# Two landing buffers each for q, k and v, requested two units ahead, in a windowed attention kernel on Trainium2

## Chip, cores and metric

One core of a Trainium2 chip. The metric is the time of one execution on the device in microseconds, measured without the profiler; smaller is better. "Before" ran in 947.35 us (median of the four runs beside the changed kernel, 946.81 to 947.8).

## The reference

Attention inside windows of 64 rows. No window sees another.

```python
B, S, D, W = 4, 4096, 1536, 64           # q, k, v: (B, S, D) float32
q_w = q.reshape(B, S // W, W, D)         # k_w, v_w the same way
logits = einsum('bnwd,bnud->bnwu', q_w, k_w) * D ** -0.5
attn = softmax(logits, axis=-1)
out = einsum('bnwu,bnud->bnwd', attn, v_w)
```

Inputs and output are 100.66 MB each, 402.65 MB in all. There is little arithmetic for each byte.

## The kernel before

The 16,384 rows are cut into N = 32 units of 512 rows (4 row slots on 128 partitions). For each unit q, k and v are loaded by GpSimd with a cast from float32 to float16 on the way, 3.146 MB read each; TensorE transposes q and k, multiplies, ScalarE takes the exponential, TensorE multiplies by v, VectorE and ScalarE scale into one of three output buffers, and GpSimd requests the store, 3.146 MB. A load lands in a landing buffer; GpSimd then copies it into `q16`, `k16` or `v16` ("hand over"), so that the landing buffer is free while TensorE works. `m_q` counts the units whose q has been transposed.

```python
ql = sb("ql", [P, SLOTS, D], FP16)            # one landing buffer for q
kl = sb("kl", [P, SLOTS, D], FP16)            # one for k
NV = 2
vls = [sb(f"vl{i}", [P, SLOTS, D], FP16) for i in range(NV)]   # two for v
# ... cut
def hand_over(src, dst, d, u, m, g):          # GpSimd
    gp.wait_ge(d, 16 * u)                     # landed
    gp.wait_ge(m, copies[0] // 3 + 1)         # dst no longer read
    gp.tensor_copy(out=dst..., in_=src...).then_inc(c_l, 1)
    copies[0] += 1
    gp.wait_ge(c_l, copies[0])
    gp.sem_inc(g, 1)                          # TensorE may start
# ... cut: SyncE requests q of unit 0 in three parts (row slot 0, slot 1, slots 2 and 3)
nc.gpsimd.wait_ge(d_r0, 16)                   # row slot 0 of q has landed
nc.gpsimd.affine_select(out=ident...)
load("k", 0, k16, d_k0)
load("v", 0, v16, d_v0)
# ... cut: q of unit 0 cast on GpSimd, q1, k1, v1, v2 requested
for u in range(1, N):
    hand_over(ql, q16, d_q, u, m_q, g_q)
    if u + 1 < N:
        load("q", u + 1, ql, d_q)
    hand_over(kl, k16, d_k, u, m_k, g_k)
    if u + 1 < N:
        load("k", u + 1, kl, d_k)
    for what in {N - 3: "", N - 2: "-v"}.get(u, "s"):      # the tail has its own order
        if what == "v":
            load("v", N - 1, vls[(N - 1) % NV], d_v[(N - 1) % NV])
        else:
            gp.wait_ge(m_q, u + 1)
            store(u - 2 if what == "-" else u - 1)
    if u == N - 2:
        store(u - 1)
    hand_over(vls[u % NV], v16, d_v[u % NV], (u + u % NV) // NV, m_v, g_v)
    if u + NV < N - 1:
        load("v", u + NV, vls[u % NV], d_v[u % NV])
# the last unit's store in two halves: one from GpSimd, one from SyncE
for h, (eng, c) in enumerate(((gp, 1), (sy, 3))):
    # ... cut: waits
    eng.dma_start(out=..., in_=...).then_inc(d_l[h], 16)
gp.drain()
# ... cut: SyncE waits for the last landings, GpSimd clears the semaphores
```

The softmax here doesn't subtract the row's maximum and nothing guards it: scores larger than these inputs give would overflow.

## Time and profile before

| | before |
|---|---|
| time | 947.35 us (median) |
| span of the profiled run | 946.4 us |
| DMA engines busy | 90% or more in 39 of 40 slices |
| TensorE, VectorE, ScalarE, GpSimd busy | 69%, 30%, 35%, 36% |
| HBM traffic | 402.65 MB, 425 GB/s over the span |

Read it from the DMA row: the engines that move the bytes hardly ever rest, those that compute do. The prediction below shows the slices and the timeline and divides the span by them. Three groups of instructions belong beside it, GpSimd's copies at the hand-overs (busy us in all, mean ns, then the idle time before them and what ended it):

```profile
L292 POOL COPY q<-ql 128x3072 f32<-128x3072 f32 x31 | 85.0, 2743 | 395.7 <-DMA ql<-in_q_dram 395.5
...
L292 POOL COPY k<-kl 128x3072 f32<-128x3072 f32 x31 | 85.3, 2751 | 110.5 <-DMA kl<-in_k_dram 110.5
...
L292 POOL COPY v<-vl 128x3072 f32<-128x3072 f32 x31 | 85.5, 2758 | 10.4 <-DMA vl<-in_v_dram 10.4
```

and the DMA issues (size, then the median time from the issue to the landing in us):

```profile
out_dram<-out POOLq DMA_DIRECT2D x31, 3072.0 KB, 32.5
ql<-in_q_dram POOLq DMA_DIRECT2D x31, 1536.0 KB, 25.8
kl<-in_k_dram POOLq DMA_DIRECT2D x31, 1536.0 KB, 25.8
vl<-in_v_dram POOLq DMA_DIRECT2D x31, 1536.0 KB, 35.7
```

GpSimd waits 395.5 us for q. That is the number that invites the change.

### The profile page before, as it was taken

The numbers are of one execution on the slowest core, as the hardware profiler recorded it, in microseconds if no ns is written. First come the engines' busy times: TensorE is split into PE (matmuls) and PEld (weight loads), VectorE is DVE, ScalarE is ACT, GpSimd is POOL, SyncE is SP. The second block draws the span as 40 slices with busy tenths as digits, with TensorE's granted clock in tenths as the row PEclk, the third lists the DMA queues.
The fourth block names the chain that finished last, engine by engine and source line by source line (L and its number), as shares of the span: only waits on it lengthen the run. The fifth ranks groups of instructions, "written<-read, shape, count | busy, mean of one in ns | idle before, by whom it ended". The sixth has DMA issues, their size and how long they took to land. (4 is left out here: it accounts for less than half of the span.)

```text
span 946.4 us, 11421 instructions
## 1 busy us (share of the span) xinstructions
PE 651.0 (69%) x4096; PEld 419.8 (44%) x3456; DVE 279.7 (30%) x453; ACT 332.8 (35%) x642; POOL 341.5 (36%) x229
## 2 busy tenths in 40 slices
PE   2776866768667676667777667866768666777682
PEld 2544543445534345434554344543435533445450
DVE  1333223332233231333313323223322233232331
ACT  1433323333334342333423334323333234343252
POOL 4323343233442334423344323343233442333520
PEclk9989777897878887798878789878898879797897
DMA  9999999999999999999999999999999999999997
GB/s 250 216 229 270 283 281 282 242 257 283 281 280 258 243 282 282 278 270 236 278 282 280 279 238 265 282 280 282 249 251 283 283 281 264 238 279 283 197 315 321
DMA packets 26940, 253.35 MB, mean 268 GB/s; under 512 B 2096, under 2 KB 2096, under 8 KB 10544
## 3 DMA queue, kind: packets, MB, share of 16 engines
q0 software_dynamic: 26352, 248.52, 100.0%
q1 hardware_dynamic: 576, 4.72, 1.3%
q14 instruction: 10, 0.08, 0.0%
q8 instruction: 2, 0.03, 0.0%
HBM read 301.99 MB, written 100.66 MB: 425 GB/s over the span
## 5 line engine op out<-in xcount | busy, mean ns | idle before, releaser
L147 PE MATMUL tp<-ident,q 128*128 128x128 f32 x768 | 165.0, 384 | 185.6 <-PEq L213 172.7
L147 PEld LDWEIGHTS tp<-ident,q 128*128 128x128 f32 x768 | 131.2, 200 | 239.4 <-issue 236.8
L292 POOL COPY q<-ql 128x3072 f32<-128x3072 f32 x31 | 85.0, 2743 | 395.7 <-DMA ql<-in_q_dram 395.5
L159 PE MATMUL lt<-xq,xk 128*128 128x256 f16 x1536 | 210.2, 288 | 0.0
L147 PE MATMUL tp<-ident,k 128*128 128x128 f32 x768 | 136.3, 317 | 67.3 <-PEq L213 54.5
L159 PEld LDWEIGHTS lt<-xq,xk 128*128 128x128 f16 x1536 | 156.8, 102 | 30.4
L222 ACT COPY xq<-tp 128x512 f32<-128x512 f32 x96 | 60.2, 627 | 291.2 <-ACTq L213 291.2
L147 PEld LDWEIGHTS tp<-ident,k 128*128 128x128 f32 x768 | 105.1, 163 | 86.3 <-issue 83.9
L222 DVE COPY xq<-tp 128x512 f32<-128x512 f32 x96 | 66.4, 692 | 254.7 <-DVEq L213 254.7
L222 ACT COPY xk<-tp 128x512 f32<-128x512 f32 x96 | 59.8, 623 | 228.6 <-ACTq L213 228.6
L222 DVE COPY xk<-tp 128x512 f32<-128x512 f32 x96 | 66.5, 693 | 198.6 <-DVEq L213 198.6
L292 POOL COPY k<-kl 128x3072 f32<-128x3072 f32 x31 | 85.3, 2751 | 110.5 <-DMA kl<-in_k_dram 110.5
L264 ACT ACTIVATE et<-lt,zeros 32x128 f16<-32x128 f32 x256 | 92.0, 359 | 39.4 <-ACTq L213 36.1
L188 PEld LDWEIGHTS <-et 128*128 128x128 f16 x384 | 30.2, 97 | 152.7 <-issue 116.7
L115 PE MATMUL o<-v,et 128*128 128x512 f16 x384 | 93.3, 379 | 0.0
L251 DVE TENSOR_SCALAR out<-o,rs 128x512 f32<-128x512 f32 x128 | 90.2, 747 | 7.7
L292 POOL COPY v<-vl 128x3072 f32<-128x3072 f32 x31 | 85.5, 2758 | 10.4 <-DMA vl<-in_v_dram 10.4
L115 PE MATMUL tp<-v,et 128*128 128x512 f16 x256 | 75.8, 377 | 0.0
L241 DVE RECIPROCAL rs<-sp 128x2 f32<-128x2 f32 x64 | 10.6, 166 | 162.6 <-DVEq L213 162.4
L275 ACT ACTIVATE out<-tp,rs 128x512 f32<-128x512 f32 x64 | 44.0, 688 | 37.2 <-ACTq L213 31.3
L251 DVE TENSOR_SCALAR out<-tp,rs 128x512 f32<-128x512 f32 x64 | 48.1, 751 | 26.2 <-DVEq L213 26.2
L115 PE MATMUL lt<-v,et 128*128 128x512 f16 x128 | 48.3, 377 | 0.0
(22 smaller groups left out, 201.2 us busy)
## 6 DMA issues: line engine op xcount, KB each, us to landing
out_dram<-out POOLq DMA_DIRECT2D x31, 3072.0 KB, 32.5
ql<-in_q_dram POOLq DMA_DIRECT2D x31, 1536.0 KB, 25.8
kl<-in_k_dram POOLq DMA_DIRECT2D x31, 1536.0 KB, 25.8
vl<-in_v_dram POOLq DMA_DIRECT2D x31, 1536.0 KB, 35.7
out<-in_q_dram SPq DMA_DIRECT2D x2, 768.0 KB, 6.5
out<-in_q_dram SPq DMA_DIRECT2D x1, 1536.0 KB, 11.2
k<-in_k_dram POOLq DMA_DIRECT2D x1, 1536.0 KB, 12.2
v<-in_v_dram POOLq DMA_DIRECT2D x1, 1536.0 KB, 18.8
```

Of the source, the lines that this page charges most:

```text
L115: return nc.tensor.add_instruction(mybir.InstMatmult(name=nc.get_next_instruction_name(), engine=PE, ins=[low(rhs), low(w)], outs=[low(o)] ...
L147: ins = nc.tensor.transpose(tps[g % 2][:, r, j, :], pairs[:, c * P : (c + 1) * P], ident[:, :])
L159: ins = nc.tensor.matmul(lts[h][:, r, :, :], lhsT=halves(xk, c)[:, r, h, :, w], rhs=halves(xq, c)[:, :, h, :, w], start=(c == 0 and w == 0 ...
L188: ld = nc.tensor.ldweights(w)
L222: copy(out=dst, in_=tps[g % 2][:, :, :, :]).then_inc(f_c[g % 4], 1)
L241: ve.reciprocal(out=rs[:, n : n + R], in_=sp[:, n : n + R]).then_inc(n_d, 1)
L251: ins = ve.tensor_scalar_mul(scaled(u, n, j), bank(n, j), scalar1=rs[:, n : n + 1])
L264: ins = sc.activation(ets[h][s, :, :, s], lts[h][s, :, :, s], EXP, bias=zeros[s, 0:1], scale=scale)
L275: ins = sc.activation(scaled(u, n, j), bank(n, j), COPY, bias=0.0, scale=rs[:, n : n + 1])
L292: gp.tensor_copy(out=dst[:, :, :].bitcast(FP32), in_=src[:, :, :].bitcast(FP32)).then_inc(c_l, 1)
```

## The change

The intent: q and k get a second landing buffer, as v has, so that a request never waits for its own buffer; with it all requests go out two units ahead in one plain order (q, k, store, v), and the tail's own order is dropped. In addition the very first transfer is half a row slot, so that GpSimd can request k and v of unit 0 sooner. Two more buffers of 12 KiB per partition are used. The core of the diff:

```diff
-    ql = sb("ql", [P, SLOTS, D], FP16)
-    kl = sb("kl", [P, SLOTS, D], FP16)
-    NV = 2
-    vls = [sb(f"vl{i}", [P, SLOTS, D], FP16) for i in range(NV)]
+    NL = 2
+    landing = {x: [sb(f"{x}l{i}", [P, SLOTS, D], FP16) for i in range(NL)] for x in "qkv"}
...
+    def request(x, u):
+        if u < N:
+            load(x, u, landing[x][u % NL], landed[x][u % NL])
...
     # hand_over(x, u, dst, m, g): waits for landed[x][u % NL], copies, and at its end:
+        request(x, u + NL)
...
-        for sl, s in ((slice(0, 1), d_r0), (slice(1, 2), d_r1), (slice(2, SLOTS), d_r2)):
-            nc.sync.dma_start(out=outs[0][:, sl, :], in_=raw[:, sl, :]).then_inc(s, 16)
+        for lo, hi, c0, c1, s in (
+            (0, 1, 0, D // 2, d_r0), (0, 1, D // 2, D, d_r1), (1, 2, 0, D, d_r2), (2, SLOTS, 0, D, d_r3)
+        ):
+            nc.sync.dma_start(
+                out=outs[0][:, lo:hi, c0:c1], in_=raw[:, lo:hi, c0:c1]
+            ).then_inc(s, 16)
...
+        for x, u in (("k", 1), ("v", 1), ("q", 2), ("k", 2), ("v", 2)):
+            request(x, u)
...
         for u in range(1, N):
+            hand_over("q", u, q16, m_q, g_q)
+            hand_over("k", u, k16, m_k, g_k)
+            gp.wait_ge(m_q, u + 1)
+            store(u - 1)
+            hand_over("v", u, v16, m_v, g_v)
     # (the loop body of before, with the tail's own order, is removed)
```

More of the change, by code (lines that the diff above doesn't have):

```diff
@@ L74 @@
     sp = ps("sp", [P, 4])
-    d_r0, d_r1, d_r2, d_q, d_k, d_k0, d_v0 = (
-        sem(n) for n in ("d_r0", "d_r1", "d_r2", "d_q", "d_k", "d_k0", "d_v0")
+    d_r0, d_r1, d_r2, d_r3, d_k0, d_v0 = (
+        sem(n) for n in ("d_r0", "d_r1", "d_r2", "d_r3", "d_k0", "d_v0")
     )
-    d_v = [sem(f"d_v{i + 1}") for i in range(NV)]
+    landed = {x: [sem(f"d_{x}{i + 1}") for i in range(NL)] for x in "qkv"}
     d_o = [sem(f"d_o{i}") for i in range(NO)]
@@ L283, in store, with hand_over @@
         ).then_inc(d_o[u % NO], 16)
+    def request(x, u):
+        if u < N:
+            load(x, u, landing[x][u % NL], landed[x][u % NL])
     copies = [0]
-    def hand_over(src, dst, d, u, m, g):
+    def hand_over(x, u, dst, m, g):
         gp = nc.gpsimd
-        gp.wait_ge(d, 16 * u)
-        gp.wait_ge(m, copies[0] // 3 + 1)
+        gp.wait_ge(landed[x][u % NL], 16 * ((u + u % NL) // NL))
+        gp.wait_ge(m, u)
         gp.tensor_copy(
-            out=dst[:, :, :].bitcast(FP32), in_=src[:, :, :].bitcast(FP32)
+            out=dst[:, :, :].bitcast(FP32), in_=landing[x][u % NL][:, :, :].bitcast(FP32)
         ).then_inc(c_l, 1)
@@ L314 @@
         for i in range(SLOTS):
-            nc.gpsimd.wait_ge((d_r0, d_r1, d_r2, d_r2)[i], 16)
+            nc.gpsimd.wait_ge((d_r1, d_r2, d_r3, d_r3)[i], 16)
             nc.gpsimd.tensor_copy(out=q16[:, i, :], in_=outs[0][:, i, :]).then_inc(c_q, 1)
             if i == 1:
-                load("q", 1, ql, d_q)
-        load("k", 1, kl, d_k)
-        for u in range(1, NV + 1):
-            load("v", u, vls[u % NV], d_v[u % NV])
+                request("q", 1)
+        for x, u in (("k", 1), ("v", 1), ("q", 2), ("k", 2), ("v", 2)):
+            request(x, u)
         nc.vector.memset(ones[:, :], 1.0).then_inc(i_d, 1)
@@ L358 @@
         for u in range(1, N):
-            hand_over(ql, q16, d_q, u, m_q, g_q)
-            if u + 1 < N:
-                load("q", u + 1, ql, d_q)
-            hand_over(kl, k16, d_k, u, m_k, g_k)
-            if u + 1 < N:
-                load("k", u + 1, kl, d_k)
-            for what in {N - 3: "", N - 2: "-v"}.get(u, "s"):
-                if what == "v":
-                    load("v", N - 1, vls[(N - 1) % NV], d_v[(N - 1) % NV])
-                else:
-                    gp.wait_ge(m_q, u + 1)
-                    store(u - 2 if what == "-" else u - 1)
-            if u == N - 2:
-                store(u - 1)
-            hand_over(vls[u % NV], v16, d_v[u % NV], (u + u % NV) // NV, m_v, g_v)
-            if u + NV < N - 1:
-                load("v", u + NV, vls[u % NV], d_v[u % NV])
+            hand_over("q", u, q16, m_q, g_q)
[3 more added lines that the diff above has]
+            hand_over("v", u, v16, m_v, g_v)
         base, o = (N - 1) * UR, outs[(N - 1) % NO]
```

## The prediction

> **What bounds the kernel now.** I read the page's slices first, then its DMA part, then GpSimd's timeline, because GpSimd issues nearly every transfer, and last the landing records.
>
> The slices of the span (tenths busy; DMA is the mean over the 16 DMA engines), then the DMA queues and the HBM traffic:
>
> ```profile
> PE   2776866768667676667777667866768666777682
> POOL 4323343233442334423344323343233442333520
> DMA  9999999999999999999999999999999999999997
> ...
> q0 software_dynamic: 26352, 248.52, 100.0%
> ...
> HBM read 301.99 MB, written 100.66 MB: 425 GB/s over the span
> ```
>
> DMA is at nine tenths or more in every slice but the last. No compute engine is near that: TensorE is at six to eight tenths. The kernel is a queue of transfers, and time is lost only where that queue is empty.
>
> How fast the queue moves is read from GpSimd's timeline. Its copy of `ql` to `q16` starts when q has landed (start, length, what; in brackets the idle time before it and who ended it):
>
> ```profile
> 823.47 2.74 POOL L292 COPY q<-ql 128x3072 f32<-128x3072 f32 x1 [13.16 <-DMA ql<-in_q_dram]
> ...
> 852.64 2.74 POOL L292 COPY q<-ql 128x3072 f32<-128x3072 f32 x1 [13.16 <-DMA ql<-in_q_dram]
> ...
> 881.80 2.75 POOL L292 COPY q<-ql 128x3072 f32<-128x3072 f32 x1 [15.18 <-DMA ql<-in_q_dram]
> 885.13 0.53 POOL L108 DMA_DIRECT2D ql<-in_q_dram  x1 [0.58 <-POOL q L292]
> 889.07 2.75 POOL L292 COPY k<-kl 128x3072 f32<-128x3072 f32 x1 [3.41 <-DMA kl<-in_k_dram]
> 892.41 0.53 POOL L108 DMA_DIRECT2D kl<-in_k_dram  x1 [0.58 <-POOL k L292]
> ...
> 920.93 2.74 POOL L292 COPY v<-vl 128x3072 f32<-128x3072 f32 x1 [7.69 <-DMA vl<-in_v_dram]
> 929.57 0.55 POOL L382 DMA_DIRECT2D out_dram<-out  x1 [5.89 <-ACT out L275]
> ```
>
> A unit takes 29.17 us (852.64 - 823.47, and again to 881.80), and is four transfers, q, k, v and the store, each 3.146 MB on the HBM side: 7.29 us each, 12.58 MB / 29.17 us = 431 GB/s. All 32 units are 128 transfers, 128 x 7.29 = 933.4 us. The span, 946.4 us, then divides so:
> - Head: q of unit 1 is the fourth transfer, and its copy starts at 34.36 us. 34.36 - 4 x 7.29 = 5.2 us.
> - Middle: from 34.36 to q of unit 30 at 881.80 lie 29 units, 845.9 us at 29.17. The rest, 1.5 us, is in five or so units near 150 to 240 and 385 to 415 us that took 29.35 to 29.76 us.
> - Tail gap: from the copy of k of unit 30 (889.07) to the copy of v of unit 31 (920.93) are 31.86 us. Between them landed q31, k31, store 28 and v31, one unit's worth, 29.17. 2.7 us too many.
> - End: after v31 come three stores. 946.4 - 920.93 - 3 x 7.29 = 3.6 us of last landings and closing.
>
> Sum: 933.4 + 5.2 + 1.5 + 2.7 + 3.6 = 946.4.
>
> **Where the tail gap comes from.** In the two lines at 885.13 and 892.41 the requests for q31 and k31 are issued. Before, q of the next unit can be requested only when the single `ql` has been copied, and the tail has its own order: unit 29 requests only q30 and k30, no store and no v. So when k30 is in transfer nothing stands behind it until q31 is requested at 885.13, and q31 is then alone until k31 at 892.41. The landing records (each transfer has 16 increments, one per DMA engine) say the same: for k31 the increments reach from 902.81 to 906.31, 3.5 us apart, where k30's were 2.9 apart, and its last comes 9.97 us after q31's last at 896.34. A transfer takes 7.29, so 2.7 us were lost on the slowest engine.
>
> **What the Trainium skill says.** "DMA: Bandwidth & Descriptors", section "Where 436 GB/s comes from", gives 435.2 GB/s as what the 16 ports carry. The trace agrees as a ceiling: 431 GB/s in the steady part is 99% of it. "HBM Reference", "Specifications (TRN2)", has about 358 GB/s as a core's share and about 425 for one streaming alone; the page's 425 over the span agrees with the latter. The first page, "Why a DMA increments its semaphore by 16 and not by 1", says only the full 16 means landed; here the last increment is 1.5 us (early) to 2.9 us (late) after the first, so the slowest engine counts. "SBUF — State Buffer", "Specifications (TRN2)", gives about 208 KiB usable per partition. The new set takes 36 (q16, k16, v16) + 6 x 12 (landing) + 24 (xq, xk) + 72 (outs) + about 2.5 = 206.5 KiB, 24 more than before; it just fits. No run shows that limit yet.
>
> **The change part by part.**
> 1. *A second buffer for q and one for k, requests two units ahead.* No transfer is added or removed, no bytes change, and the cyclic order in the queue stays q, k, store, v. In the steady part the queue was never empty: on landing of q(u) there stood k, store and v behind it, 22 us. Seven transfers, 51 us, will stand there now. The rate is the ceiling's, so gain 0 x 31 units. Time from request to landing must rise. Before, q: four transfers less the copy and the gap before the issue, 4 x 7.29 - 3.4 = 25.8 us, which is the page's 25.8. After: 8 x 7.29 - 3.4 = 54.9 us for q, k and v, and about 32.5 + 29.2 = 61.7 for the store.
> 2. *The tail without its own order.* The last requests become q30, k30, store 27, v30, q31, k31, store 28, v31, store 29, store 30, store 31. q31 and k31 are requested when q29 and k29 have been copied, some 55 us ahead, so the gap goes: -2.7 us. Three stores still follow v31. Does the queue run dry before the last one? Before, the first half of store 31 is issued 929.57 - 920.93 = 8.6 us after the copy of v31 starts; stores 29 and 30 give 14.6 us of work. No gap, before or after: 0.
> 3. *The store's later place.* store(u-1) now stands in front of v(u+2), and unit u+2 is the next that writes that output buffer (three buffers). It lands a transfer, 7.3 us, ahead of v(u+2), without which those outputs can't start: 0.
> 4. *The first transfer halved.*
>
> ```profile
> 0.96 1.33 SPq L303 DMA_DIRECT2D out<-in_q_dram  x3
> ...
> 6.98 0.28 POOL L307 TENSOR_SCALAR_AFFINE_SELECT ident<-ident 128x128 f32<-128x128 f32 x1 [6.54 <-DMA out<-in_q_dram]
> 7.51 0.68 POOL L108 DMA_DIRECT2D k<-in_k_dram  x1 [0.24 <-issue]
> ```
>
> GpSimd waits for the first row slot before it requests k and v of unit 0. A slot is a quarter transfer, 1.8 us; with half of it the wait ends about 0.9 us earlier and k is issued near 6.6. But the first loads of q keep the engines until 10.4 us (first landing of the last of them), and k's first packets start at 10.0 us. Only a shallow dip around 10.5 us can be filled, and on the slowest engine perhaps nothing: I take -0.2 us. A fourth issue on SyncE and packets of half the size may take that back.
>
> Sum: 0 - 2.7 + 0 - 0.2 = -2.9 us. 947.6 - 2.9 = 944.7 us.
>
> **Rivals.**
> - *The wait for q is the cost.* GpSimd's wait for `ql` is 395.5 us over 30 units, the largest of all waits, and two landing buffers look made for it. If it were on the path, a few us per unit would go and the time would fall by tens of us, to 850 or 900. Against it: during that wait the DMA engines move 431 GB/s. The wait is GpSimd waiting for bytes that are on their way. I expect it to move to `vl`, not to shrink: per unit q waits 7.3 - 4.1 = 3.2, k 3.4, v 14.6 - 4.6 = 10 us; so some 100, 105 and 300 us in total.
> - *The gap is moved, not removed.* The engines that ran ahead gain, and the one that is last was never idle. The landing records speak against it (its k31 took 9.97), but the lag of the slowest engine grew by 1.4 us over the run where single packets were held up, and can grow otherwise. Then 946.5 to 947.5.
> - *GpSimd blocks.* Eight transfers outstanding instead of four: if the room for descriptors is short, an issue (0.54 to 0.72 us now) grows and copies come late. The prologue already had six outstanding with issues of 0.7 us. A unit's compute takes about 21 us of 29.2 (unit 0 started at 16.4 and unit 1 at 37.6), so up to 8 us per unit are hidden. Only more than that would cost: 960 or more, unlikely.
> - *More compute beside transfers slows them.* Units 1 and 2 come without stores, 21.9 us apart, so compute runs closer together for a moment. The middle's total would change by less than a us.
>
> **Range and chances.** The sure term is the tail gap, 2.7 us, which can't exceed 0.3% of the time; the head is worth -0.7 to +0.5; the drift in the middle, 1.5 us now, may be 0.5 to 3. So 943.0 to 947.0 in 8 of 10. 2% is 19 us: nothing found here can give that, as 933.4 us are bytes at the ceiling; for slower I leave the blocked GpSimd.
>
> **What would show it.** In the profile after: unit spacing still 29.16 to 29.17 us; landing times near 55 (loads) and 62 us (store); the wait moved from `ql` to `vl`; from the landing of k30 to that of v31 about 29.2 us instead of 31.9; k of unit 0 issued near 6.6 us, and q of unit 1 landed within 0.5 us of before. It is wrong if the unit spacing changes by over 0.1 us, if issues on GpSimd grow, or if the spacing at the end stays above 31 us.

## The result, and the profile after

The changed kernel took 943.89 us (median of 4, 942.61 to 944.69) against 947.35: ratio 0.9963, 95% interval 0.9945 to 0.998. Repeated later with six runs it took 944.71 us against 946.5, ratio 0.9977 (0.9965 to 0.9989). Ratios and their 95% intervals are from the runs of the same rounds; they are not quite the ratios of the medians or of the means. By the threshold of 2% the two kernels count as the same; the intervals say that the small gain is outside the noise. The output is correct.

The same views after. The slices and queues:

```profile
DMA  9999999999999999999999999999999999999998
...
q0 software_dynamic: 26352, 248.52, 100.4%
...
HBM read 301.99 MB, written 100.66 MB: 428 GB/s over the span
```

Packets and bytes of the queue are unchanged to the last one. The hand-overs' waits and the issues:

```profile
L294 POOL COPY v<-vl 128x3072 f32<-128x3072 f32 x31 | 85.2, 2747 | 295.9 <-DMA vl<-in_v_dram 295.9
...
L294 POOL COPY q<-ql 128x3072 f32<-128x3072 f32 x31 | 85.0, 2742 | 110.3 <-DMA ql<-in_q_dram 110.3
L294 POOL COPY k<-kl 128x3072 f32<-128x3072 f32 x31 | 85.2, 2747 | 106.9 <-DMA kl<-in_k_dram 106.9
```

```profile
out_dram<-out POOLq DMA_DIRECT2D x31, 3072.0 KB, 61.8
ql<-in_q_dram POOLq DMA_DIRECT2D x31, 1536.0 KB, 54.9
kl<-in_k_dram POOLq DMA_DIRECT2D x31, 1536.0 KB, 54.9
vl<-in_v_dram POOLq DMA_DIRECT2D x31, 1536.0 KB, 54.9
```

The wait for q fell from 395.5 to 110.3 us and the one for v rose from 10.4 to 295.9: 285.2 us less, 285.5 us more. A request for q or k now takes 54.9 us from its issue to its landing instead of 25.8. e1 below shows that the time hardly depends on either.

GpSimd's timeline at the end (start, length; in brackets the idle time before):

```profile
836.90 2.74 POOL L294 COPY q<-ql 128x3072 f32<-128x3072 f32 x1 [3.19 <-DMA ql<-in_q_dram]
...
866.06 2.74 POOL L294 COPY q<-ql 128x3072 f32<-128x3072 f32 x1 [3.20 <-DMA ql<-in_q_dram]
873.33 2.75 POOL L294 COPY k<-kl 128x3072 f32<-128x3072 f32 x1 [4.53 <-DMA kl<-in_k_dram]
...
917.15 2.74 POOL L294 COPY v<-vl 128x3072 f32<-128x3072 f32 x1 [10.51 <-DMA vl<-in_v_dram]
```

The unit spacing is 29.16 us as before. From k30 to v31 are 43.82 us, now six transfers (store 27, v30, q31, k31, store 28, v31): 6 x 7.29 = 43.75. Before, it was 31.86 us for four.

I divide the span of each profiled run the same way. One transfer is 29.166 / 4 = 7.2915 us, 128 of them 933.3 us. "Head" is the start of q1's copy less four transfers. "Middle" is from there to q30's copy, less its transfers (116 before, 114 in the changed order). "Tail" is from k30's copy to the last landing in the trace's landing records, less its transfers (7 before, 9 after). "Closing" is from the last landing to the end of the span. In us:

| profiled run | head | middle | tail | closing | span |
|---|---|---|---|---|---|
| before | 5.2 | 1.6 | 2.8 | 3.5 | 946.4 |
| changed, first | 5.7 | -0.1 | 0.1 | 1.8 | 940.8 |
| changed, again (e0) | 5.4 | 0.5 | 0.4 | 3.2 | 942.9 |

The first trace of the changed kernel is that of its fastest run, and its closing is short. In the second the closing is nearly as long as before. The tail is short in both.

### The profile page after: what moved, and what is told of

Same layout as the page of the kernel before. It is cut to its first block, busy times and chain, and to the rows that moved or that the text cites. A ratio compares the mean times of both kernels' runs of the same rounds, so it can differ in the third digit from the quotient of the medians.

```text
span 940.8 us, 11422 instructions
## 1 busy us (share of the span) xinstructions
PE 659.4 (70%) x4096; PEld 396.2 (42%) x3456; DVE 280.2 (30%) x453; ACT 335.6 (36%) x642; POOL 340.9 (36%) x229
## 5 line engine op out<-in xcount | busy, mean ns | idle before, releaser
L157 PE MATMUL lt<-xq,xk 128*128 128x256 f16 x1536 | 215.5, 292 | 0.0
L145 PE MATMUL tp<-ident,k 128*128 128x128 f32 x768 | 148.5, 337 | 83.4 <-PEq L211 73.4
L294 POOL COPY v<-vl 128x3072 f32<-128x3072 f32 x31 | 85.2, 2747 | 295.9 <-DMA vl<-in_v_dram 295.9
L145 PE MATMUL tp<-ident,q 128*128 128x128 f32 x768 | 110.8, 291 | 69.0 <-DVE xq L220 36.5
L145 PEld LDWEIGHTS tp<-ident,k 128*128 128x128 f32 x768 | 114.7, 175 | 103.3 <-issue 100.8
L186 PEld LDWEIGHTS <-et 128*128 128x128 f16 x384 | 35.0, 109 | 285.8 <-issue 280.3
L145 PEld LDWEIGHTS tp<-ident,q 128*128 128x128 f32 x768 | 90.1, 149 | 109.1 <-issue 108.4
L294 POOL COPY q<-ql 128x3072 f32<-128x3072 f32 x31 | 85.0, 2742 | 110.3 <-DMA ql<-in_q_dram 110.3
L113 PE MATMUL o<-v,et 128*128 128x512 f16 x384 | 116.2, 448 | 0.0
L113 PE MATMUL sp<-ones,et 128*128 128x1 f16 x256 | 25.8, 170 | 116.6 <-PEq L211 114.3
L113 PE MATMUL tp<-v,et 128*128 128x512 f16 x256 | 92.8, 450 | 0.0
L113 PE MATMUL lt<-v,et 128*128 128x512 f16 x128 | 58.2, 455 | 0.0
## 6 DMA issues: line engine op xcount, KB each, us to landing
out_dram<-out POOLq DMA_DIRECT2D x31, 3072.0 KB, 61.8
ql<-in_q_dram POOLq DMA_DIRECT2D x31, 1536.0 KB, 54.9
kl<-in_k_dram POOLq DMA_DIRECT2D x31, 1536.0 KB, 54.9
vl<-in_v_dram POOLq DMA_DIRECT2D x31, 1536.0 KB, 54.9
```

Source lines behind the costliest of these rows:

```text
L113: return nc.tensor.add_instruction(mybir.InstMatmult(name=nc.get_next_instruction_name(), engine=PE, ins=[low(rhs), low(w)], outs=[low(o)] ...
L145: ins = nc.tensor.transpose(tps[g % 2][:, r, j, :], pairs[:, c * P : (c + 1) * P], ident[:, :])
L157: ins = nc.tensor.matmul(lts[h][:, r, :, :], lhsT=halves(xk, c)[:, r, h, :, w], rhs=halves(xq, c)[:, :, h, :, w], start=(c == 0 and w == 0 ...
L186: ld = nc.tensor.ldweights(w)
L294: gp.tensor_copy(out=dst[:, :, :].bitcast(FP32), in_=landing[x][u % NL][:, :, :].bitcast(FP32)).then_inc(c_l, 1)
```

## Experiments

Theory G: the gain is the gap at the end, where before's queue ran short. Rivals: D, the deeper queue saves time in the middle; C, the closing is shorter. Times are medians; "against before" is the difference of the means of the runs in the same rounds.

| run | time | against before | head | middle | tail | closing |
|---|---|---|---|---|---|---|
| e0 changed, again | 944.71 | -2.1 | 5.4 | 0.5 | 0.4 | 3.2 |
| e1 before, tail filled | 944.51 | -2.4 | 5.2 | 1.3 | 1.0 | 2.6 |
| e2 changed, no half | 945.12 | -1.7 | 6.2 | 1.6 | 0.1 | 3.2 |
| e3 changed, queue emptied | 952.93 | +5.8 | 5.5 | 0.4 | 8.4 | 2.7 |
| e4 before, with half | 947.60 | +0.1 | 6.2 | 2.1 | 1.7 | 3.5 |
| e5 before, SyncE tail | 945.33 | -2.1 | 5.0 | 1.1 | 2.2 | 1.3 |
| e6 changed, SyncE tail | 942.91 | -4.6 | 6.3 | 0.3 | 0.1 | 1.4 |
| e7 transfers only | 946.66 | -1.0 | | | | |
| e8 changed, no head wait | 944.58 | -3.1 | 5.8 | 0.3 | 0.1 | 3.1 |
| e9 changed, no warm-up | 944.93 | -2.5 | 5.5 | 1.0 | 1.0 | 3.6 |
| e10 changed, SyncE tail, no half | 943.48 | -4.1 | 5.9 | 0.9 | 0.3 | 1.4 |

### e0, the changed kernel again

> The changed kernel as it is, again, to measure the difference with more runs and to see a second trace of it. In its first profiled run four terms stood against before: head +0.5 us, drift in the middle -1.5, tail gap -2.7, closing after the last landing -1.8. Theory G (the tail gap is the cause): 3 to 4 us faster than before, the trace has k30's copy to v31's copy in 43.7 to 43.9 us (six transfers, no gap). If drift and closing are chance, they differ in this trace: drift 0 to 1.5, closing 1.7 or 3.5. Rival D (depth in the middle is the cause): drift is again 0. Rival C (closing is the cause): closing is again 1.7.

2.1 us faster than before, less than the 3 to 4 expected (one of the eleven runs of before, 949.98 us, lies apart; without it the difference is 1.8). From k30's copy to v31's copy it took 44.16 us, a little over the 43.7 to 43.9 expected. The middle and the closing did differ from the first trace (0.5 and 3.2); the tail is 0.4, still far from before's 2.8. So rival C can't carry the whole gain: with a closing only 0.3 us shorter than before most of it is still there.

### e1, only the tail of the kernel before filled

```diff
+    qx, kx: one more landing buffer for q and for k, used by the last unit alone
             if u + 1 < N - 1:
                 load("k", u + 1, kl, d_k)
+            if u == N - 3:
+                load("q", N - 1, qx, d_qx)
+                load("k", N - 1, kx, d_kx)
```

> The kernel before, with one buffer each for q and k as before, but q and k of the last unit have buffers of their own and are requested a unit earlier, right behind k30. Only the empty queue at the end is taken away; the depth in the other 30 units is as before. Theory G: 2.7 us faster than before (2.2 to 3.2), that is within 1 us of the changed kernel; k30's copy to v31's copy 29.2 us instead of 31.9. Rival D: at most 1 us faster than before, as the middle is unchanged. Rival C: no change in the time unless the closing changes.

GpSimd's timeline of this run, the two copies that bound one unit's four transfers:

```profile
888.77 2.75 POOL L295 COPY k<-kl 128x3072 f32<-128x3072 f32 x1 [4.53 <-DMA kl<-in_k_dram]
...
918.33 2.74 POOL L295 COPY v<-vl 128x3072 f32<-128x3072 f32 x1 [4.28 <-DMA vl<-in_v_dram]
```

29.56 us, where before it was 31.86. The time is 2.4 us less than before and within 0.3 us of the changed kernel in the same rounds. Thirty of the 31 requests for q, and of those for k, were as late as before. So rival D is not needed: two requests of 62 bring as much as the whole change, within the noise (about 1 us).

### e2, the changed kernel without the halved first transfer

```diff
-            (0, 1, 0, D // 2, d_r0), (0, 1, D // 2, D, d_r1), (1, 2, 0, D, d_r2), (2, SLOTS, 0, D, d_r3)
+            (0, 1, d_r0), (1, 2, d_r2), (2, SLOTS, d_r3)
```

> The changed kernel with the first transfer whole again, a full row slot. If the halving gains what the prediction gave it (0.2 us): this is 0.2 us slower than the changed kernel; q1's copy starts 0.2 us later than 34.9. The first trace of the changed kernel says otherwise: the wait for the first half ended at 6.97 us, against 6.98 for the whole slot before. So I now expect no difference beyond 0.3 us, k of unit 0 requested at 7.5 us in both, and perhaps q1 0.5 us EARLIER, as before (34.36).

945.12 us against 944.71 with the half in the same rounds; by means 0.5 us apart, more than the 0.3 expected, but the two intervals overlap (0.9968 to 0.9993 and 0.9965 to 0.9989). k of unit 0 was requested at 7.78 us, against 7.21 in e0, not at the same time. q1's copy started at 35.37, not earlier: that guess missed. No use of the half is shown here; e4 and e8 look further.

### e3, the queue emptied on purpose

```diff
-        request(x, u + NL)
+        if u + NL != N - 1:
+            request(x, u + NL)
...
+            if u == N - 2:          # after v30 has been copied
+                request("q", N - 1); request("k", N - 1)
+                store(u - 2); request("v", N - 1); store(u - 1)
```

> The changed kernel with the queue emptied on purpose near the end: q31, k31, store 28, v31 and store 29 are requested only after v30 has been copied. The gap is a term that can be doubled: after the last landing of v30 come the copy (2.8 us), the gap before the issue (0.6) and the first packets (about 2): 5.2 to 6 us with nothing in transfer. Theory G (an empty queue is paid in full): 5 to 6.5 us slower than the changed kernel, so 2 to 3 us slower than before. A rival in which a gap on the queue is partly caught up later (engines ahead wait for the last one anyway): 2 to 4 us slower than the changed kernel.

It cost more than either expectation: 952.93 us, 7.9 us above the changed kernel by means. The windows of this run (window, its length, busy time of PE, PEld, DVE, ACT, POOL, granted clock, DMA share, GB/s) say why:

```profile
886.00:888.00 2.00, 0.95 (x9) 0.58 (x6) 0.00 (x0) 1.76 (x5) 0.00 (x0) 1.00 0.26 52
888.00:890.00 2.00, 0.00 (x0) 0.00 (x0) 0.00 (x0) 1.11 (x4) 1.75 (x1) 1.00 0.00 0
890.00:892.00 2.00, 0.81 (x5) 0.16 (x3) 0.00 (x0) 0.00 (x0) 1.40 (x2) 0.80 0.00 0
892.00:894.00 2.00, 2.00 (x7) 0.30 (x2) 0.43 (x2) 0.60 (x1) 2.00 (x4) 0.50 0.78 98
894.00:896.00 2.00, 2.00 (x12) 0.32 (x4) 1.09 (x2) 1.18 (x3) 0.80 (x2) 0.84 0.89 184
```

About 5 us carry nothing (the last packets start before 887.5, the first new ones after 892), as reckoned. But then the engines are busy and slow: 98 GB/s where loads of q and k run at some 216 (GB/s counts bytes written). In the packet records the packets that start from 892 to 894 take 1.55 to 1.62 us on average instead of 0.926. The tail in the table gives 8.4 us for the whole, so some 3 us more are lost after the transfers start again (an estimate: 8.4 less 5). The packet records show packets of 1.50 to 1.55 us a second time, from 906 to 909 us, although all five requests had been out since 894.8 us; so it is not only the first packets that are slow. The kernel before shows slow packets at its gap too:

```profile
882.00:885.50 3.50, 0.61 (x3) 0.64 (x4) 0.00 (x0) 0.00 (x0) 2.92 (x2) 0.59 1.06 225
885.50:888.00 2.50, 2.37 (x12) 1.96 (x11) 0.69 (x1) 0.62 (x1) 0.16 (x1) 0.50 0.86 147
...
894.00:897.00 3.00, 3.00 (x29) 2.73 (x28) 0.69 (x1) 0.63 (x1) 3.00 (x3) 1.00 0.95 152
897.00:900.00 3.00, 3.00 (x29) 2.62 (x28) 0.69 (x1) 0.63 (x1) 2.77 (x2) 1.00 0.93 187
```

There the DMA share hardly dips, 0.86 and 0.95, but the GB/s fall to 147 and 152. So the gap was mostly slow packets; idle was some 0.7 us (an estimate: what the shares 0.86, 0.95 and 0.93 lack to 1, times their windows). Nor was the queue quite empty. By the landing records the first engine ended k30 at 886.08, 0.95 us after the request for q31, and q31 at 894.60, 2.19 us after the request for k31; packets were slow after both. Why they are slow no run shows.

### e4, the kernel before with the halved first transfer alone

> The kernel before with only the halved first transfer of the change. The prediction gave the halving 0.2 us. After the repeat of the changed kernel and the one without the half (944.7 and 945.1), I expect 0 to 0.4 us faster than before, that is nothing that these rounds can tell from zero; the wait for the first half ends at 6.4 to 7.0 us, when the slowest DMA engine is done, as the whole slot's did.

The edit is the change's four-part request put into the kernel before. 947.60 against 947.51 us, ratio 0.9999 (0.9986 to 1.0013); the first half's last increment came at 6.84 us and k was requested at 7.67. No gain of the halving is shown; with an interval of over 1 us to either side this run could not show the predicted 0.2.

### e5 and e6, both halves of the last store from SyncE

```diff
-        for h, (eng, c) in enumerate(((gp, 1), (sy, 3))):
+        for h, (eng, c) in enumerate(((sy, 1), (sy, 3))):
```

> The kernel before, with both halves of the last store issued by SyncE instead of one by GpSimd and one by SyncE. In six traces so far the clearing of the semaphores starts 2.30 to 2.39 us after GpSimd's own half has landed, whichever half lands last. Theory K (GpSimd's drain after its own last transfer costs 2.3 us): here GpSimd's last own transfer is store 30, which lands some 6 us before the end, so the clear comes within 0.6 us of the last landing, and the time from the last landing to the end falls from 3.5 to 1.6-1.8 us: 1.5 to 2 us faster than before. Rival (the closing has a fixed length and the short one of the changed kernel's first trace was chance): no difference.

> The changed kernel with both halves of the last store issued by SyncE. Theory K: its closing is always 1.6 to 1.8 us, 1.0 to 1.6 us less than in the repeat of the changed kernel (3.2), so about 943.4 us and about 3.2 us faster than before. If this also beats the kernel before with the same edit by about 2.3 us, the two terms add.

Both came as theory K has it, a little better than expected. The closings are 1.33 and 1.35 us. The clearing of the semaphores follows the last landing by 0.13 us, where with GpSimd's half it came 2.30 to 2.39 us after that half had landed, in all ten traces that have one. That GpSimd's half is the cause is shown; that the drain is what takes the time is argued, as no run takes it out. In the first trace of the changed kernel GpSimd's half landed at 937.23 and SyncE's at 939.04: the 2.4 us ran beside the other half, and so its closing was short. e5 is 2.1 us faster than before, e6 4.6 (ratio 0.9951, 0.9938 to 0.9965): the two terms add, and e6 beats the kernel before. The changed kernel was not run in e6's rounds, and the intervals of their ratios touch or overlap (0.9945 to 0.998 and 0.9965 to 0.9989 for the changed kernel); that e6 is faster than it too rests on the closing in the traces of e5, e6 and e10.

### e7, the transfers alone

The changed kernel without compute and without GpSimd's hand-over copies; its output is wrong.

> Gives a wrong result on purpose: the changed kernel's transfers alone, in the same order and with the same buffers, without TensorE's, VectorE's and ScalarE's work and without GpSimd's copies. It is the floor that any order of these transfers has. If the kernel is bound by its transfers in every part, this takes 941 to 944.5 us, 0 to 3 us less than the changed kernel. A rival in which compute beside the transfers slows them (by its traffic, or by late requests): 930 us or less.

946.66 us, above the expected range and above the changed kernel of other rounds. It was run on another chip. Compute beside the transfers therefore costs nothing that this can show; the rival's 930 us is far off. The landing records say where the surplus is: the spread of one transfer's 16 increments grows from 1.7 us to 4.6 over the run, as two engines fall back (in the changed kernel's first trace it stays at 1.8 to 2.3), and the end waits for the last: 14 engines had ended by 937.51 us, the other two at 941.60 and 942.09. A cost of compute below that surplus could hide behind it. Why those engines fell back further here is open. Its head is of use too:

```profile
4.90 0.28 POOL L310 TENSOR_SCALAR_AFFINE_SELECT ident<-ident 128x128 f32<-128x128 f32 x1 [4.45 <-DMA out<-in_q_dram]
5.43 0.68 POOL L106 DMA_DIRECT2D k<-in_k_dram  x1 [0.24 <-issue]
```

Here the wait for the half slot ends at 4.9 us and k is requested 2 us earlier than in the full program. The changed kernel has

```profile
6.97 0.28 POOL L315 TENSOR_SCALAR_AFFINE_SELECT ident<-ident 128x128 f32<-128x128 f32 x1 [6.52 <-DMA out<-in_q_dram]
7.49 0.68 POOL L106 DMA_DIRECT2D k<-in_k_dram  x1 [0.25 <-issue]
```

which is 6.97 against 6.98 for the whole slot before. In the landing records 15 of the half's increments are there at 4.47 us and the sixteenth comes at 6.67. The half was early on all engines but one.

### e8, no wait ahead of the first k and v

```diff
         nc.gpsimd.wait_ge(i_d, 1)
-        nc.gpsimd.wait_ge(d_r0, 16)
...
+        nc.gpsimd.wait_ge(d_r0, 16)     # just before the copies that need it
         for i in range(SLOTS):
```

> The changed kernel without GpSimd's wait in front of k and v of unit 0: they are requested at about 1.5 to 2.5 us instead of 7.2 to 7.5; the wait for the half slot moves to just before the copy that needs it. It is the change's fourth part driven to its end. Theory Q (the engines are busy with the first q until 10.4 us, so an earlier request gains nothing): the copy of q1 starts within 0.4 us of 34.9 and the time is within 0.6 us of the changed kernel. Rival (the request's lateness costs): q1 up to 2 us earlier and the time 1 to 2 us shorter.

```profile
1.99 0.68 POOL L106 DMA_DIRECT2D k<-in_k_dram  x1 [0.25 <-issue]
...
35.00 2.75 POOL L294 COPY q<-ql 128x3072 f32<-128x3072 f32 x1 [5.49 <-DMA ql<-in_q_dram]
```

k is requested 5.5 us earlier and q1's copy starts at 35.0 us, as in the changed kernel (34.89 and 34.61). The time is 944.58 us. Theory Q holds: the engines are full with q of unit 0, and an earlier request only puts k in among it. The last half of q of unit 0 was cast from 23.66 us on, where in the changed kernel it was from 15.82.

### e9, no warm-up of ScalarE's table

```diff
-        nc.scalar.activation(zeros[:, 3:4], zeros[:, 0:1], EXP, bias=zeros[:, 0:1], scale=1.0)
```

> The changed kernel without ScalarE's first small exponential, which makes it load its table at the start. In the run with transfers alone the first half slot landed on all engines by 4.60 us, in all runs with the whole program one engine was last at 6.4 to 6.9 us; the 16,384-byte fetch on queue 8 (about 1.1 us) and the instruction fetches on queue 14 fall on that time. If the table's fetch is what holds that engine: the last increment of the first half comes at 5.3 us or before and k is requested by 6.2. If it is the instruction fetches: no change there. In both cases no difference of the whole time beyond 0.6 us, as the request isn't what counts.

The last increment of the first half came at 6.42 us, as in e0 (6.38); the 16,384-byte fetch at 4.2 us was still there, so the edit did not take away what it was to test. What holds that one engine is not settled: in e7, where it isn't held, both that fetch and the instruction fetches at that time are missing. The time is unmoved, 944.93 us.

### e10, the candidate

> Candidate for the best version: the changed kernel with both halves of the last store issued by SyncE and with the first transfer whole. If the halving is worth nothing, it takes the same as the one with the half, 942.5 to 943.5 us, some 4.5 us less than before.

943.48 us, ratio 0.9957 (0.9943 to 0.997), inside the range. It was run with other rounds than e6, and their intervals overlap, so the half makes no difference that is shown. Either is the best version here.

## Why the prediction was right

It said 944.7 us in 943.0 to 947.0; measured were 943.89 and, again, 944.71.

- *The wait for q is not the cost.* Right. It went to v as laid out (100, 105 and 300 us expected; 110, 107 and 296 measured), at an unchanged unit spacing of 29.16 us, and the times to landing, 54.9 and 61.8, were met within 0.1 us. The transfers alone (e7) are no faster. GpSimd's issues stayed at 0.53 to 0.75 us, so the rival in which GpSimd blocks did not come.
- *The tail gap.* Right in cause: e1 and e3 take the gap away and enlarge it, and the time follows. In size, one trace's 2.7 us was a little high: from k30 to the last landing the kernels with before's tail lose 2.8, 1.7 and 2.2 us (before, e4, e5), those with the changed order 0.05 to 1.0, so about 2 us on average are won. And it is not what I pictured as an empty queue: mostly slow packets. One sign was worked out wrongly: in the order that the prediction itself gives, six transfers lie between the landings of k30 and v31, not four, so "about 29.2 us" should have been 43.75 (43.82 and 44.16 measured), and "stays above 31 us" taken by its words would have called it wrong.
- *The queue doesn't run dry before the last stores.* Right: the tail of the changed order loses 0.1 us or less in four of its seven traces (e3 left out), and 1.0 at most.
- *The head, -0.2 us.* The step "with half of it the wait ends about 0.9 us earlier and k is issued near 6.6" failed. k was issued at 7.49, because the wait ends with the slowest engine, and that one was held till 6.67 us whatever was asked of it. The argument behind it, that the engines are busy with q anyway, held (e8). "q of unit 1 landed within 0.5 us of before" holds in one trace of two (0.25 and 0.53 us later).
- *End, 3.6 us unchanged.* Not named as a term that could move, yet it was 1.8 in one trace and 3.2 in the other, by how long before SyncE's half of the last store GpSimd's had landed (1.8 and 0.4 us). That is 1.4 us of scatter as large as half the gain. Over the traces with GpSimd's half the closing is 3.0 us on average in the changed order (five, e3 left out) and 3.5 in both with before's tail, so some tenths of the gain may lie here.
- *Middle.* Over the traces with the full program the drift is 1.1 to 2.1 us in before's order and -0.1 to 1.6 in the changed order, while the head is somewhat longer in the latter. On average (four and seven traces, e3 left out) the middle is 0.9 us shorter and the head 0.4 us longer. Whether two units ahead saves some tenths there stays open; e1, with the depth of before, is as fast. The slow units that the prediction puts near 150 to 240 and 385 to 415 us lie between 122 and 210 and between 356 and 415.
- *Luck.* That 944.71 meets 944.7 is luck in part: the tail won less than predicted, the head lost instead of winning, and middle and end, both put at no change, made it up.
- *Room in SBUF.* The 206.5 KiB per partition that the prediction adds up did fit: the kernel built and ran correctly.

## What to carry to other kernels

Ask of a long wait whether the resource that it waits for is idle meanwhile; here 395 us of waiting were worth nothing, and two requests at the end were worth 2 us. In a kernel bound by transfers, follow the queue's content to the last request: here 5 us without transfers cost 8.4 us (e3), and requests that came 1 to 2 us before the first engine had ended its work still cost 2 to 3 us. A wait for a transfer is a wait for the slowest of its 16 engines, so a smaller first piece helps only if that engine isn't held by something else.

## What the Trainium skill lacked or had wrong

- "DMA: Bandwidth & Descriptors", in its section "Anatomy of one DMA — SWDGE (gpsimd) path", gives a fixed cost of about 2 us for a transfer. Not there: after the queue has run short or empty, packets are slow as well. In e3 the first ones took 1.55 to 1.62 us instead of 0.926, and a stretch of 5 us without transfers cost 8.4 us.
- The same page says, under "Why a DMA increments its semaphore by 16 and not by 1", that only the full 16 means that all has landed, and, under "Latency and other measured facts", that two of the engines are usually slower. Not there: how far the engines drift apart in a long run and that the lag stays. The spread was about 1.5 to 3.0 us in the kernel before, up to its tail, and up to 4.6 us in e7, there by two engines. The packet records here don't name the engines, so whether they are the page's two is not shown.
- No page has what it costs at the end when GpSimd issues a last transfer: the clear behind its drain came 2.30 to 2.39 us after that transfer's landing in ten traces, and 0.13 to 0.14 us after the last landing when SyncE had issued the last transfers.
